# Chunk scores: levels computed on halves of TensorE's columns, both groups of heads in one step, scores kept head-innermost

## The chip, the core and the metric

One core of one Trainium2 chip runs the kernel. The metric is device time in microseconds, the median of several runs; one further execution was taken with the hardware profiler. Five engines work beside each other, each through its own queue in order: TensorE (PE, with its weight loads PEld), VectorE (DVE), ScalarE (ACT), GpSimd (POOL) and the queue engine SP. They wait for one another by semaphores.

## What is computed

One layer of a hybrid decoder: a gated linear recurrence (HGRN2) beside a gated short convolution, one output projection, then a gated MLP with a causal convolution. The change touches the recurrence's scores:

```python
def hgrn2_chunkwise(q, k, v, log_f):
    def step(state, inp):
        qc, kc, vc, gc = inp
        b = jnp.cumsum(gc, axis=-2)
        diff = b[..., :, None, :] - b[..., None, :, :]
        decay = jnp.exp(jnp.where(causal[:, :, None], diff, -jnp.inf))
        scores = jnp.einsum('bhtk,bhsk,bhtsk->bhts', qc, kc, decay)
        o = (jnp.einsum('bhts,bhsv->bhtv', scores, vc)
             + jnp.einsum('bhtk,bhkv->bhtv', qc * jnp.exp(b), state))
        ...
```

There are 4 heads of 128 features, 1024 tokens and 1024 model columns; everything is fp32.

## The kernel before

The 1024 tokens go through in two halves `hf` of 512, each half in four chunks of C = 128 tokens. The big products are split in two parts of a number (`hi`, `lo`, float32r) and done as three matmuls of 128x512 each (`mm3_fm`, `mm3_tm`, lines 177 to 185). A product of `gemm_quad` or `gemm_tile` is a run of such matmuls, and every 24 of them (or 12, by the `rate` argument) the helper `tick` takes one step out of the deque `fill` and records it there. So the scores and the recurrence (`score_steps`, `chunk_steps`) are recorded in small steps between the big matmuls. A scheduling layer then orders each engine's instructions; the order below is the one that it made.

`UW` holds keys and queries of the four chunks as (chunk parity `x`, key or query `s`, two groups `g` of four heads, token), `F` the decays, `S` the scores. Group g of parity x is chunk 2g + x. The scores are built without logarithms: `diag` (line 348) fills the diagonal, and then seven levels with block sizes h = 1, 2, 4, ... 64 (`LEVELS`) fill the blocks of h left tokens by h right tokens. Before each level `prepare` (line 364) gathers on ACT, into a tile `lhs`, the left keys of the even chunk and the right queries of the odd chunk, so that one matmul per head (line 380) serves both parities; the odd chunk's scores come out transposed. Then, on DVE: line 382 and line 384 multiply the blocks of `UW` with decays for the next level, line 386 merges the decays in `F`, and line 387 copies, where the mask `m_lev` says so, the wanted scores from PSUM into `S`. The next level's `prepare` needs lines 382 and 384, and its matmuls need `prepare`'s copy.

A level is done per group g: two steps `level(li, 0)` and `level(li, 1)`, each with its own matmuls (4 heads, 128 left columns by 128 moving columns), its own copies, and an `lhs` of 128x512 that has two buffers. So while one group's chain runs on DVE and ACT, the other group's matmuls and 12 to 24 big matmuls stand between on PE. After the levels, `scores` (in `chunk_steps`) transposes the odd chunks' scores by TensorE, and `output` multiplies scores and state with values and queries. PSUM tiles for all this come from a ring of four banks (`aux`). The masks are loaded by two DMAs on SP's queue and converted on POOL.

Of the kernel before, what the change touches and what calls it, by code (L numbers as in the profile page):

```python
# [38 lines left out]
N_MASK = C + C * len(LEVELS)  # L39
# [3 lines left out]
def decoder_kernel(ctx: ExitStack, tc: tile.TileContext, x, xT, w_sq, w_cv, w_out, w_up, w_dn,  # L43
# [24 lines left out]
    m_lev = zp.tile([P, len(LEVELS), 2, H, 64], U8, name="m_lev")  # L68
# [38 lines left out]
    def aux(name, shape=(P, TH)):  # L107
        return ps_ax.tile(list(shape), F32, tag="ax", name=name)
# [127 lines left out]
    S = zt("S", (P, 2, 8, C))  # L236
# [99 lines left out]
    def score_steps(hf, F, UW):  # L336
        kq = {}

        def products(xi, g):
            gs = slice(g * H, (g + 1) * H)  # L340
            p = cv(f"kq{hf}_{xi}_{g}", shape=(P, H, C))
            nc.vector.tensor_tensor(p[:], UW[:, 2 * xi, gs, :], UW[:, 2 * xi + 1, gs, :], ALU.mult)
            hi = cv(f"kqh{hf}_{xi}_{g}", F32R, (P, H, C))
            lo = cv(f"kql{hf}_{xi}_{g}", F32R, (P, H, C))
            split(p[:], hi[:], lo[:])
            kq[xi, g] = hi, lo

# [16 lines left out]
        def prepare(li, g):  # L364
            h = LEVELS[li]
            lhs = zt("lhs", (P, H, C), bufs=2, name=f"lhs{hf}_{li}_{g}")
            nc.scalar.copy(lhs.rearrange("p i (b two h) -> p (i b) two h", two=2, h=h),  # L367
                           view(UW, 4 * X, g * H * C, (2 * h, H * C // (2 * h)), (3 * X + h, 2), (1, h)))
            lhss[li, g] = lhs

        def level(li, g):
            h = LEVELS[li]
            nb = C // (2 * h)
            ps = aux(f"sl{hf}_{li}_{g}")
            lhs = lhss.pop((li, g))
            pv = ps.rearrange("p (x g b h) -> p x g b h", x=2, g=H, h=h)
            o, n = g * H * C, H * nb
# [3 lines left out]
            u = view(UW, 4 * X, o, (3 * X + h, 2), (2 * h, n), (1, h))  # L381
            nc.vector.tensor_tensor(u, u, view(F, 2 * X, o + h, (X - h, 2), (2 * h, n), (0, h)), ALU.mult)
            w = view(UW, 4 * X, X + o + h, (X - h, 2), (2 * h, n), (1, h))
            nc.vector.tensor_tensor(w, w, view(F, 2 * X, o, (X + h, 2), (2 * h, n), (0, h)), ALU.mult)  # L384
            left = view(F, 2 * X, o, (X, 2), (2 * h, n))
            nc.vector.tensor_tensor(left, left, view(F, 2 * X, o + h, (X, 2), (2 * h, n)), ALU.mult)
            nc.vector.copy_predicated(
                view(S, 2 * X, o + h, (X - h, 2), (2 * h, n), (1, h)),
                m_lev[:, li].rearrange("p x g (b h) -> p x (g b) h", h=h),
                ps.rearrange("p (x n h) -> p x n h", x=2, h=h))  # L390
# [8 lines left out]
        lg = [(li, g) for li in range(len(LEVELS)) for g in range(2)]  # L399

        steps = [chain((products, *xg[0]))] + [chain()] * (2 * hf)
        for i in range(4):
            steps.append(chain((diag, *xg[i]), *([(products, *xg[i + 1])] if i < 3 else []),
                               *([(prepare, 0, i // 2)] if i % 2 else [])))
        for li, g in lg:
            steps.append(chain((level, li, g), *([(prepare, li + 1, g)] if li + 1 < len(LEVELS) else [])))
# [5 lines left out]
    def chunk_steps(hf, F, UW, v, gg, ma):  # L412
        ma_hi, ma_lo = ma

        def make(c):
# [8 lines left out]
            def scores():  # L424
                ps = aux(f"so{n}", (P, H, C))
                for j, ph, _ in hs:
                    nc.tensor.transpose(ps[:, j, :], S[:, 1, ph, :], ident[:])
                nc.scalar.copy(S[:, 1, g * H : (g + 1) * H, :], ps[:])

            def output():  # L430
# [8 lines left out]
                for _, ph, js in hs:  # L439
                    if not first:  # L440
                        nc.tensor.matmul(po[:, js], Q[:, ph, :], st[0][:, js], start=True, stop=False)
                    nc.tensor.matmul(po[:, js], S[:, xi, ph, :], v[c][:, js], start=first, stop=True)
# [87 lines left out]
    def out_proj(hf, mix, gain, hooks=None):  # L530
# [46 lines left out]
        for nh in range(2):  # L577
            if nh and hf:
                for c in range(NC_H):
# [3 lines left out]
                            hooks=hooks if nh == 0 else None, rate=1 + (hf == 0))  # L583
# [81 lines left out]
    for i in range(2):  # L665
        mf = xslot(f"mf{i}")
        nc.sync.dma_start(mf[:], masks_d[:, i * TH : (i + 1) * TH])
        mv = mf.rearrange("p (l x n) -> p l x n", x=2, n=64)
        if i == 0:
            nc.gpsimd.tensor_copy(m_diag[:], mf[:, 0:C])  # L670
        for l in range(1 - i, 4):
            nc.gpsimd.tensor_copy(m_lev[:, 4 * i + l - 1], mv[:, l].unsqueeze(2).to_broadcast([P, 2, H, 64]))
# [14 lines left out]
    mix_a = mixers(0, act_a, F0, UW0, rb0, rq0, r0, ma_tiles(0), ((1, 2, 1, 2), (1, 2, 1, 2)), (2, 1, 2, 1, 2, 1, 2, 1, 2, 1, 2, 1),  # L687
# [14 lines left out]
    mix_b = mixers(1, act_b, F1, UW1, rb1, rq1, r1, ma_tiles(1), (2, 2), (1, 1, 1, 1, 1, 1, 1, 1, 1, 1, 2, 2))  # L702
# [510 lines left out]
```

## Time and profile before

| | us |
|---|---|
| median of 3 runs (1108.78 to 1110.8) | 1109.32 |
| profiled execution | 1109.08 |
| its span in the trace | 1107.3 |
| PE busy | 1095.9 |
| DVE busy | 826.9 |
| ACT busy | 514.3 |
| POOL busy | 14.0 |

The span is the time that the trace covers; some 1.8 us of the execution lie around it. A matmul is pipelined: its record lasts until its last result is modelled to have landed, so the records overlap, and what a matmul really takes is the distance from its start to the next one's start. An fp32 matmul is two records (two weight loads and two matmuls), a float32r matmul or an fp32 transpose one. A row "x8" merges eight records, with the first one's start and the time from there to the last one's end.

### The profile page before, as it was taken

What the parts mean: (1) busy time and instruction counts of PE and PEld (TensorE: products, weight loads), DVE (VectorE), ACT (ScalarE), POOL (GpSimd) and SP (SyncE); (2) the same over time, 40 slices, a digit from 0 to 9 for tenths busy, and PEclk for the clock granted to TensorE, in tenths of its full rate; (3) what the DMA queues carried; (4) which work ended last, traced back from release to release, by engine and by line L of the source; (5) the groups of instructions that cost most, each with busy time, mean ns of one, the idle gap of its engine ahead of it and who ended that gap; (6) DMA issues with size and microseconds to landing.
All of it is one profiled execution on the core that took longest, in us unless ns stands there. A gap on an engine that the chain in (4) does not pass through costs nothing.

```text
span 1107.3 us, 13513 instructions
## 1 busy us (share of the span) xinstructions
PE 1095.9 (99%) x5088; PEld 911.5 (82%) x5088; DVE 826.9 (75%) x1196; ACT 514.3 (46%) x769; POOL 14.0 (1%) x25
## 2 busy tenths in 40 slices
PE   9999999999999999999999999999999999999996
PEld 7888888887888888888888888888888888888885
DVE  7576877658954666388698888889888767855776
ACT  5543355433433337277444554445454434544541
POOL 2000000000000001000000000000000000000000
PEclk9999999999999999999999999999999999999999
DMA  9522223322352348075333333443432479877632
GB/s 297 193 95 76 77 76 126 116 98 70 101 185 96 96 131 271 27 256 176 128 130 137 133 124 128 157 162 107 158 115 86 136 257 408 319 249 234 208 105 107
DMA packets 56161, 170.38 MB, mean 154 GB/s; under 512 B 5656, under 2 KB 6176, under 8 KB 53152
## 3 DMA queue, kind: packets, MB, share of 16 engines
q1 hardware_dynamic: 54880, 165.50, 42.8%
q0 software_dynamic: 912, 3.67, 1.0%
q8 instruction: 40, 0.66, 0.2%
q10 hardware_dynamic: 304, 0.35, 0.1%
q14 instruction: 25, 0.20, 0.1%
HBM read 134.11 MB, written 35.39 MB: 153 GB/s over the span
## 4 chain that ended last, share of the span: by engine, by line
PE 94%; DVE 3%; issue 1%; ACT 1%; DMA 0%; DVEq 0%; SPq 0%; ACTq 0%
PE pG L178 7%; PE pG L180 7%; PE pG L179 7%; PE pV L178 4%; PE pV L180 4%; PE pV L179 4%; PE pX L183 3%; PE pX L185 3%; PE pX L184 3%; PE pY L183 3%; PE pY L184 3%; PE pY L185 3%; PE p_wo L183 2%; PE p_wo L184 2%; PE p_wo L185 2%; PE sl L380 2%
## 5 line engine op out<-in xcount | busy, mean ns | idle before, releaser
L117 DVE TENSOR_TENSOR ls<-s,hs 128x1024 fp32r<-128x1024 f32 (+1 forms) x40 | 45.1, 1129 | 46.1 <-ACT hs L116 46.1
L116 ACT CAST hs<-s 128x1024 fp32r<-128x1024 f32 (+1 forms) x40 | 39.1, 977 | 78.6 <-PE pY L184 28.8
L776 DVE TENSOR_TENSOR l_t<-t,h_t 128x1536 fp32r<-128x1536 f32 x22 | 38.6, 1754 | 32.3 <-ACT h_t L775 32.3
L775 ACT CAST h_t<-t 128x1536 fp32r<-128x1536 f32 x22 | 32.6, 1483 | 55.3 <-PE pG L179 55.3
L875 ACT ACTIVATE g<-g 128x1024 f32<-128x1024 f32 x22 | 23.4, 1062 | 64.8 <-DVE g L863 64.8
L185 PE MATMUL pY<-hw,ls 128*128 128x512 f32 x132 | 51.4, 389 | 0.0
L184 PE MATMUL pY<-lw,hs 128*128 128x512 f32 x132 | 51.3, 389 | 0.0
L183 PE MATMUL pY<-hw,hs 128*128 128x512 f32 x132 | 51.2, 389 | 0.0
L184 PE MATMUL pX<-lw,hs 128*128 128x512 f32 x116 | 45.1, 389 | 0.0
L183 PE MATMUL pX<-hw,hs 128*128 128x512 f32 x116 | 45.1, 389 | 0.0
L185 PE MATMUL pX<-hw,ls 128*128 128x512 f32 x116 | 45.1, 389 | 0.0
L367 ACT COPY lhs<-UW 128x512 f32<-128x512 f32 x28 | 18.6, 666 | 44.5 <-DVE UW L384 37.9
L861 ACT ACTIVATE g<-pG,vec 128x1024 f32<-128x1024 f32 x22 | 24.5, 1114 | 29.0 <-PE pG L180 29.0
L180 PE MATMUL pG<-uhi,l_x 128*128 128x512 f32 x96 | 37.4, 389 | 0.0
L178 PE MATMUL pG<-uhi,h_x 128*128 128x512 f32 x96 | 37.3, 389 | 0.0
L179 PE MATMUL pG<-ulo,h_x 128*128 128x512 f32 x96 | 37.3, 389 | 0.0
L862 DVE SCALAR_TENSOR_TENSOR g<-pG,vec,g 128x1023 f32<-128x1023 f32 x22 | 28.1, 1279 | 8.8 <-ACT g L861 8.8
L178 PE MATMUL pG<-c4h,h_b 128*128 128x512 f32 x88 | 34.3, 390 | 0.0
L179 PE MATMUL pG<-c4l,h_b 128*128 128x512 f32 x88 | 34.3, 390 | 0.0
L179 PE MATMUL pV<-c1l,h_t 128*128 128x512 f32 x88 | 34.3, 389 | 0.0
L178 PE MATMUL pV<-c1h,h_t 128*128 128x512 f32 x88 | 34.2, 389 | 0.0
L179 PE MATMUL pG<-c2l,h_t 128*128 128x512 f32 x88 | 34.2, 389 | 0.0
(361 smaller groups left out, 3410.1 us busy)
## 6 DMA issues: line engine op xcount, KB each, us to landing
w<-w_up SPq DMA_DIRECT2D x21, 1024.0 KB, 4.8
b<-w_dn SPq DMA_DIRECT2D x35, 512.0 KB, 7.1
s<-s_d SPq DMA_DIRECT2D x33, 512.0 KB, 6.2
s_d<-g SPq DMA_DIRECT2D x22, 512.0 KB, 2.7
s_d<-S SPq DMA_DIRECT2D x11, 768.0 KB, 3.4
r_wo<-w_out SPq DMA_DIRECT2D x16, 512.0 KB, 3.5
ah_w<-w_up SPq DMA_DIRECT2D x10, 512.0 KB, 4.9
f_d<-ah_f SPq DMA_DIRECT2D x9, 512.0 KB, 2.9
```

The lines of the kernel that those rows point to most:

```text
L116: nc.scalar.copy(hi, src)
L117: nc.vector.tensor_tensor(lo, src, hi.bitcast(F32), ALU.subtract)
L178: nc.tensor.matmul(ps, whi, ahi, start=first, stop=False, skip_group_check=more)
L179: nc.tensor.matmul(ps, whi, alo, start=False, stop=False, skip_group_check=more)
L180: return nc.tensor.matmul(ps, wlo, ahi, start=False, stop=last, skip_group_check=more)
L183: nc.tensor.matmul(ps, ahi, whi, start=first, stop=False, skip_group_check=more)
L184: nc.tensor.matmul(ps, ahi, wlo, start=False, stop=False, skip_group_check=more)
L185: return nc.tensor.matmul(ps, alo, whi, start=False, stop=last, skip_group_check=more)
L775: m = nc.scalar.copy(hi[:], src)
L776: casts[name] = m.ins, nc.vector.tensor_tensor(lo[:], src, hi[:].bitcast(F32), ALU.subtract).ins
L861: nc.scalar.mul(a[:], c, wc[2])
L862: nc.vector.scalar_tensor_tensor(a[:, 1:], c[:, : T - 1], wc[1], a[:, 1:], ALU.mult, ALU.add)
```

## The change

A level handles all 8 heads in one step. Its matmuls are cut in two: left columns 0 to 63 against the 64 moving columns that belong to them, and left columns 64 to 127 against theirs, each placed on its own half of the array's columns (`tile_position=(0, 0)` and `(0, 64)`), in alternation. So a level has 16 matmuls of 64 by 64 where two steps had 8 of 128 by 128. Their results land in PSUM with the head innermost, one column every 8 elements. `S` is (token, head) too, the masks are cut to half a row, and line 387's copy becomes two, one on each half of the partitions. For h = 64 the copy is two plain ones on ACT. `lhs` is one buffer of 128x1024. Before the odd chunks' transposes, three ACT copies per half put the scores back in head order (`even`, `odd`). The rates at which steps are taken are set anew: 12 score steps per half instead of 19 (without the empty ones).

```diff
-    m_lev = zp.tile([P, len(LEVELS), 2, H, 64], U8, name="m_lev")
+    m_lev = zp.tile([P, len(LEVELS) - 1, 2, W // 2, GH], U8, name="m_lev")
...
-    S = zt("S", (P, 2, 8, C))
+    S = zt("S", (P, 2, C, GH))
...
-            p = cv(f"kq{hf}_{xi}_{g}", shape=(P, H, C))
-            nc.vector.tensor_tensor(p[:], UW[:, 2 * xi, gs, :], UW[:, 2 * xi + 1, gs, :], ALU.mult)
+            p = cv(f"kq{hf}_{xi}_{g}", shape=(P, C, H))
+            nc.vector.tensor_tensor(
+                p.rearrange("p t i -> p i t"), UW[:, 2 * xi, gs, :], UW[:, 2 * xi + 1, gs, :], ALU.mult)
...
-        def prepare(li, g):
+        def prepare(li):
             h = LEVELS[li]
-            lhs = zt("lhs", (P, H, C), bufs=2, name=f"lhs{hf}_{li}_{g}")
...
+            lhss[li] = zt("lhs", (P, GH, C), name=f"lhs{hf}_{li}")
...
-            for i in range(H):
-                rhs = view(UW, 4 * X, X + o + i * C + h, (X - h, 2), (2 * h, nb), (1, h))
-                nc.tensor.matmul(pv[:, :, i], lhs[:, i, :], rhs, start=True, stop=True)
...
+            halves = [slice(w * W, (w + 1) * W) for w in range(2)]
+            for i in range(GH):
+                for w, ws in enumerate(halves):
+                    if h < W:
+                        rhs = view(UW, 4 * X, X + i * C + w * W + h, (X - h, 2), (2 * h, W // (2 * h)), (1, h))
+                    else:
+                        rhs = view(UW, 4 * X, X + i * C + (h, X)[w], (1, h))
+                    nc.tensor.matmul(ps[ws, ..., i], lhs[:, i, ws], rhs, start=True, stop=True, tile_position=(0, w * W))
...
+                    nc.vector.copy_predicated(
+                        to, m_lev[ws, li].rearrange("p x (b h) i -> p x b (h i)", h=h),
+                        ps[ws].rearrange("p x (b h) i -> p x b (h i)", h=h))
+                else:
+                    nc.scalar.copy(S[ws, w, (1 - w) * W : (2 - w) * W], ps[ws])
...
-        for li, g in lg:
-            steps.append(chain((level, li, g), *([(prepare, li + 1, g)] if li + 1 < len(LEVELS) else [])))
+        for li in range(len(LEVELS)):
+            steps.append(chain((level, li), *([(prepare, li + 1)] if li + 1 < len(LEVELS) else [])))
...
+                if c == 1:
+                    shared["even"] = zt("lhs", (P, GH, C), name=f"even{hf}")
+                    for gi in range(G):
+                        shared[gi] = cv(f"odd{hf}_{gi}", shape=(P, H, C))
+                        nc.scalar.copy(shared[gi].rearrange("p i t -> p t i"), S[:, 1, :, gi * H : (gi + 1) * H])
+                    nc.scalar.copy(shared["even"].rearrange("p i t -> p t i"), S[:, 0])
...
-        gg = evac_g(hf, gemm_quad(w_sq[3], act, f"g{hf}", True, PAIRS, rate=(2, 1, 2, 1)), r)
+        gg = evac_g(hf, gemm_quad(w_sq[3], act, f"g{hf}", True, PAIRS, rate=rates[1]), r)
...
-    mix_a = mixers(0, act_a, F0, UW0, rb0, rq0, r0, ma_tiles(0), ((1, 2, 1, 2), (1, 2, 1, 2)), (2, 1, 2, 1, 2, 1, 2, 1, 2, 1, 2, 1),
+    mix_a = mixers(0, act_a, F0, UW0, rb0, rq0, r0, ma_tiles(0), (1, (1, 1, 1, 2)), (1, 1, 1, 2, 1, 2, 1, 2, 1, 2, 2, 2),
...
-    mix_b = mixers(1, act_b, F1, UW1, rb1, rq1, r1, ma_tiles(1), (2, 2), (1, 1, 1, 1, 1, 1, 1, 1, 1, 1, 2, 2))
+    mix_b = mixers(1, act_b, F1, UW1, rb1, rq1, r1, ma_tiles(1), (1, 2), (1, 2, 1, 1, 2, 1, 1, 2, 1, 1, 2, 1))
```

How this moves instructions is shown at one place on three engines, the convolution stage of the first half. PE first (`sl` is the scores' PSUM tile, `p_ch` and `p_gb` are results of the convolution's products); before:

```order
L180 MATMUL p_ch_0_985<-hi_7_308,l_ch_0_981 128x512
L380 MATMUL sl_4_1_1010<-UW_392,lhs_4_1_963 128x2x64 x4
L178 MATMUL p_gb_0_1036<-hi_0_135,h_gb_0_1031 128x512
L179 MATMUL p_gb_0_1036<-lo_0_136,h_gb_0_1031 128x512
L180 MATMUL p_gb_0_1036<-hi_0_135,l_gb_0_1032 128x512
```

and now, where the sixth level comes in the same product:

```order
L182 MATMUL p_gb_0_1065<-lo_2_186,h_gb_0_1060 128x512
L183 MATMUL p_gb_0_1065<-hi_2_185,l_gb_0_1061 128x512
L387 MATMUL sl_5_1026<-UW_392,lhs_5_990 64x64 x16
L181 MATMUL p_gb_0_1065<-hi_3_206,h_gb_0_1060 128x512
L182 MATMUL p_gb_0_1065<-lo_3_207,h_gb_0_1060 128x512
```

A group of 4 has become one of 16, and the group stands inside a product instead of at its end. Between the levels of the first half stand 24, 26, 19, 19, 17 and 15 big matmuls now, in the second half 24, 24, 22, 22, 22 and 24 (and 6 more inside the level h = 8, after its ninth matmul). Before, from a group's level to its next, there were 24 to 48 and the other group's matmuls.

DVE at the levels h = 8 and 16 of the first half (`l_gc` is the low part of a weight, `gc` the convolution's gate); before:

```order
L492 TENSOR_TENSOR gc_0_976<-gc_0_976,rb_368 128x512
L382 TENSOR_TENSOR UW_392<-UW_392,F_115 128x2x32x8
L387 COPY_PREDICATED S<-m_lev,sl_3_1_954 128x2x32x8
L384 TENSOR_TENSOR UW_392<-UW_392,F_115 128x2x32x8
L117 TENSOR_TENSOR l_gc_1_1090<-r_gc_1_1088,h_gc_1_1089 128x1024
L386 TENSOR_TENSOR F_115<-F_115 128x2x32
L387 COPY_PREDICATED S<-m_lev,sl_4_0_965 128x2x16x16
```

and now:

```order
L389 TENSOR_TENSOR UW_392<-UW_392,F_115 128x2x64x8
L399 COPY_PREDICATED S<-m_lev,sl_3_905 64x2x4x64
L391 TENSOR_TENSOR UW_392<-UW_392,F_115 128x2x64x8
L399 COPY_PREDICATED S<-m_lev,sl_3_905 64x2x4x64
L393 TENSOR_TENSOR F_115<-F_115 128x128
L513 TENSOR_TENSOR gc_0_992<-p_gc_0_943,rb_368 128x512
L389 TENSOR_TENSOR UW_392<-UW_392,F_115 128x2x32x16
```

The multiplications are twice as long and a score copy stands between the two that the next `prepare` needs; there is no second group's work between the levels. ACT at the same place, before:

```order
L116 CAST h_gb_0_1031<-r_gb_0_1030 128x1024
L367 COPY lhs_4_0_913<-UW_392 128x512
L116 CAST h_gc_1_1089<-r_gc_1_1088 128x1024
L367 COPY lhs_4_1_963<-UW_392 128x512
L367 COPY lhs_5_0_974<-UW_392 128x512
L116 CAST h_ch_1_1132<-r_ch_1_1131 128x1024
```

and now:

```order
L119 CAST h_gb_0_1060<-r_gb_0_1059 128x1024
L371 COPY lhs_3_891<-UW_392 128x1024
L119 CAST h_gc_1_1118<-r_gc_1_1117 128x1024
L371 COPY lhs_4_927<-UW_392 128x1024
L119 CAST h_ch_1_1170<-r_ch_1_1169 128x1024
L371 COPY lhs_5_990<-UW_392 128x1024
```

Each level has one `prepare` of double width, with a weight's cast between two of them.

## Rows read from the trace of the kernel before

**Rows 1.** The page: span, busy time of each engine with its share of the span, the granted clock of TensorE in 40 slices (9 is full), and the shares of the chain that ended last.

```profile
span 1107.3 us, 13513 instructions
PE 1095.9 (99%) x5088; PEld 911.5 (82%) x5088; DVE 826.9 (75%) x1196; ACT 514.3 (46%) x769; POOL 14.0 (1%) x25
...
PEclk9999999999999999999999999999999999999999
...
PE 94%; DVE 3%; issue 1%; ACT 1%; DMA 0%; DVEq 0%; SPq 0%; ACTq 0%
```

**Rows 2.** The view of waits, for PE: who waited for whom, us in total, times, the longest.

```profile
PE sl L380 <- DVE UW L384: 1.4, 4, 0.4
PE pw L80 <- DVE pr L497: 1.0, 1, 1.0
PE pZ L184 <- DVE lw L117: 0.5, 1, 0.5
```

**Rows 3.** PE's timeline around the first level group of the first half: start, time to the end of the last record, line, output<-inputs, weights' rows*columns, shape.

```profile
74.28 0.39 PE L184 MATMUL p_i<-l_i,hi 128*128 128x512 f32 x1
74.51 0.39 PE L185 MATMUL p_i<-h_i,lo 128*128 128x512 f32 x1
74.73 1.07 PE L380 MATMUL sl<-UW,lhs 128*128 128x128 f32 x8
75.56 0.48 PE L183 MATMUL p_g<-h_g,hi 128*128 128x512 f32 x1
75.87 0.40 PE L184 MATMUL p_g<-l_g,hi 128*128 128x512 f32 x1
76.11 0.40 PE L185 MATMUL p_g<-h_g,lo 128*128 128x512 f32 x1
...
296.07 1.05 PE L380 MATMUL sl<-UW,lhs 128*128 128x128 f32 x8
```

**Rows 4.** The tile `sl`: all its weight loads and matmuls, with duration ns min/median/max.

```profile
L380 PEld LDWEIGHTS sl<-UW,lhs x224: 186/191/192, 74.5 to 307.6; 128*128 128x128 f32 x112
L380 PE MATMUL sl<-UW,lhs x224: 270/275/353, 74.7 to 307.7; 128*128 128x128 f32 x112
```

**Rows 5.** PE's timeline at the statistics of the first half: eight records with 128 weight columns and one moving column (`pc<-ones,acc`), and a transpose whose weights are 4 columns (`pc<-ident,rs_x`), which the program places on a strip of 32 columns of the array. Then the line of that transpose, with its weight load.

```profile
29.26 0.39 PE L180 MATMUL p_q<-hi,l_q 128*128 128x512 f32 x1
29.49 0.95 PE L649 MATMUL pc<-ones,acc 128*128 128x1 f32 x8
30.30 0.49 PE L178 MATMUL p_q<-hi,h_q 128*128 128x512 f32 x1
30.62 0.40 PE L179 MATMUL p_q<-lo,h_q 128*128 128x512 f32 x1
...
32.48 0.40 PE L178 MATMUL p_q<-hi,h_q 128*128 128x512 f32 x1
32.71 0.27 PE L279 MATMUL pc<-ident,rs_x 128*4 128x128 f32 x1
32.74 0.47 PE L179 MATMUL p_q<-lo,h_q 128*128 128x512 f32 x1
33.05 0.39 PE L180 MATMUL p_q<-hi,l_q 128*128 128x512 f32 x1
...
L279 PEld LDWEIGHTS pc<-ident,rs_x x1: 83/83/83, 32.5 to 32.5; 128*4 128x4 f32 x1
```

**Rows 6.** The timeline of all engines from one level group (h = 8, group 0 of the first half) to the next `prepare`; in brackets the idle time before, and who ended it.

```profile
102.92 1.05 PE L380 MATMUL sl<-UW,lhs 128*128 128x128 f32 x8
103.73 0.48 PE L178 MATMUL p_gc<-hi,h_gc 128*128 128x512 f32 x1
...
104.01 0.69 DVE L382 TENSOR_TENSOR UW<-UW,F 128x512 f32<-128x512 f32 x1 [2.94 <-PE sl L380]
104.62 0.70 DVE L387 COPY_PREDICATED S<-m_lev,sl 128x512 f32<-128x512 uint8 x1
105.22 0.68 DVE L384 TENSOR_TENSOR UW<-UW,F 128x512 f32<-128x512 f32 x1
105.82 1.22 DVE L117 TENSOR_TENSOR l_gb<-r_gb,h_gb 128x1024 fp32r<-128x1024 f32 x1
105.99 0.62 ACT L367 COPY lhs<-UW 128x512 f32<-128x512 f32 x1 [1.24 <-DVE UW L384]
106.95 0.26 DVE L386 TENSOR_TENSOR F<-F 128x64 f32<-128x64 f32 x1
```

**Rows 7.** The timeline where PE waited for a level's operands.

```profile
81.66 0.39 PE L184 MATMUL p_g<-l_g,hi 128*128 128x512 f32 x1
81.79 0.69 DVE L384 TENSOR_TENSOR UW<-UW,F 128x512 f32<-128x512 f32 x1
81.89 0.39 PE L185 MATMUL p_g<-h_g,lo 128*128 128x512 f32 x1
82.63 1.15 PE L380 MATMUL sl<-UW,lhs 128*128 128x128 f32 x8 [0.36 <-DVE UW L384]
```

**Rows 8.** Single lines: duration ns min/median/max of DVE's multiplications and score copies (the longest of line 387 are those of h = 1 and 2), and of ACT's copies and casts.

```profile
L357 DVE TENSOR_TENSOR UW<-UW,F x4: 1218/1224/1226, 57.8 to 250.0; 128x1024 f32<-128x1024 f32 x4
L387 DVE COPY_PREDICATED S<-m_lev,sl x28: 699/732/1309, 76.5 to 309.3; 128x512 f32<-128x512 uint8 x28
L367 ACT COPY lhs<-UW x28: 612/621/872, 59.3 to 301.9; 128x512 f32<-128x512 f32 x28
L428 ACT COPY S<-so x4: 570/581/585, 138.1 to 355.5; 128x512 f32<-128x512 f32 x4
L116 ACT CAST h_gc<-r_gc x8: 1045/1045/1055, 89.3 to 380.5; 128x1024 fp32r<-128x1024 f32 x8
```

**Rows 9.** Stretches of time: busy us of PE, PEld, DVE, ACT and POOL (instructions), granted clock, DMA share, GB/s. The two stretches hold the levels of the first and of the second half.

```profile
74.00:137.00 63.00, 62.64 (x329) 52.99 (x329) 48.35 (x75) 21.99 (x30) 0.00 (x0) 1.00 0.23 76
257.00:308.00 51.00, 49.97 (x273) 42.27 (x272) 46.88 (x83) 21.15 (x41) 0.00 (x0) 1.00 0.30 98
```

More of the change, by code (lines that the diff above doesn't have):

```diff
@@ L38 @@
 V_N = V_FCONV + 3 * 2 * NF
-N_MASK = C + C * len(LEVELS)
+G = 2
+GH = G * H
+W = C // 2
+N_MASK = C + W * (len(LEVELS) - 1)
 @with_exitstack
@@ new lines, in prepare, with level @@
+            lhss[li] = zt("lhs", (P, GH, C), name=f"lhs{hf}_{li}")
+            nc.scalar.copy(lhss[li].rearrange("p i (b two h) -> p (i b) two h", two=2, h=h),
+                           view(UW, 4 * X, 0, (2 * h, X // (2 * h)), (3 * X + h, 2), (1, h)))
+        def level(li):
+            h = LEVELS[li]
+            n = X // (2 * h)
+            ps = aux(f"sl{hf}_{li}", (P, 2, W // 2, GH) if h < W else (P, W, GH))
+            lhs = lhss.pop(li)
+            halves = [slice(w * W, (w + 1) * W) for w in range(2)]
[6 more added lines that the diff above has]
+                    nc.tensor.matmul(ps[ws, ..., i], lhs[:, i, ws], rhs, start=True, stop=True, tile_position=(0, w * W))
+            u = view(UW, 4 * X, 0, (3 * X + h, 2), (2 * h, n), (1, h))
+            nc.vector.tensor_tensor(u, u, view(F, 2 * X, h, (X - h, 2), (2 * h, n), (0, h)), ALU.mult)
+            w = view(UW, 4 * X, X + h, (X - h, 2), (2 * h, n), (1, h))
+            nc.vector.tensor_tensor(w, w, view(F, 2 * X, 0, (X + h, 2), (2 * h, n), (0, h)), ALU.mult)
+            left = view(F, 2 * X, 0, (X, 2), (2 * h, n))
+            nc.vector.tensor_tensor(left, left, view(F, 2 * X, h, (X, 2), (2 * h, n)), ALU.mult)
+            for w, ws in enumerate(halves):
+                if h < W:
+                    sv = S[ws]
+                    to = bass.AP(tensor=sv.tensor, offset=sv.offset + (w * W + h) * GH,
+                                 ap=[list(sv.ap[0]), [X - h * GH, 2], [2 * h * GH, W // (2 * h)], [1, h * GH]])
+                    nc.vector.copy_predicated(
[3 more added lines that the diff above has]
+                    nc.scalar.copy(S[ws, w, (1 - w) * W : (2 - w) * W], ps[ws])
@@ L403, in score_steps @@
             steps.append(chain((diag, *xg[i]), *([(products, *xg[i + 1])] if i < 3 else []),
[L404 to L406 removed]
+                               *([(prepare, 0)] if i == 3 else [])))
+        for li in range(len(LEVELS)):
+            steps.append(chain((level, li), *([(prepare, li + 1)] if li + 1 < len(LEVELS) else [])))
         return steps
@@ L441, in output @@
                         nc.tensor.matmul(po[:, js], Q[:, ph, :], st[0][:, js], start=True, stop=False)
-                    nc.tensor.matmul(po[:, js], S[:, xi, ph, :], v[c][:, js], start=first, stop=True)
+                    nc.tensor.matmul(po[:, js], shared[("even", "odd")[xi]][:, ph, :], v[c][:, js], start=first, stop=True)
                 ssq = small(f"sso{n}")
```

68 lines of the change are left out of this document (23 added, 45 removed).

## The prediction

> **What bounds the kernel now.** I read the page first: PE is busy for 1095.9 of 1107.3 us at the full clock, and the chain that ended last is 94% PE [rows 1]. Then the waits of PE, longest first: the top of the list is 1.4 us, and it is the levels' matmuls that waited for DVE's second multiplication; the next are 1.0 and 0.5 [rows 2]. So PE hardly ever stands still, and every microsecond of TensorE work that goes or comes is a microsecond of the kernel, unless a new wait takes its place. Third, PE's timeline around one level group: what it costs, from start to start. Fourth, the score stages' stretches, to see how much room DVE has: 48.35 busy of 63 us in the first half and 46.88 of 51 in the second [rows 9], 77% and 92%. ACT has 21.99 and 21.15, so it is not short of room. The profiled execution is 1109.08 us against the median of 1109.32, so I work out a difference and take it from 1109.3.
>
> **Level matmuls, removed.** A group of eight records starts at 74.73 and the next matmul at 75.56: 0.83 us. That next one takes 0.31 to its successor (75.56 to 75.87) where the ordinary step is 0.23 (74.51 less 74.28): 0.08 more [rows 3]. 28 groups x 0.91 = 25.5 us, all on PE and so all on the path.
>
> **Level matmuls, added.** 14 levels of 16 matmuls, 32 records each. What does a record of 64 columns by 64 take? Within a group the starts of the seven steps lie (1.07 - 0.275) / 7 = 0.114 us apart [rows 3, 4]. Eight records with a single moving column stand equally close, 0.81 us in all against 0.83 [rows 5], so it is the load of 128 weight columns that sets this pace, at least as much as the stream of 128 moving ones. A load of 4 columns lasts 83 ns, one of 128 lasts 191 [rows 4, 5]: 0.87 ns a column, so 64 columns fewer save 0.056 us and a record stands alone at about 0.058 us. The moving columns are halved too.
>
> The open question is whether the two halves of the array work side by side. The trace has no two matmuls on different columns, so I bound it by the rows above. Fully side by side, two records pass in 0.058: 31 x 0.029 + 0.03 (the step to the next matmul, 0.83 - 7 x 0.114) + 0.08 = 1.01 us a level, 14.1 us in all, **a gain of 11.4**. In turns: 31 x 0.058 + 0.11 = 1.91 a level, 26.7 us, a loss of 1.2. I take side by side: the change alternates the halves record pair by record pair, left and right have their own weights, moving columns and PSUM partitions, and already now loads and matmuls overlap freely (a load of 191 ns every 114).
>
> Two things could add to a record. The first is changing between the whole array and halves, 28 times. The 4-column transpose stands on a strip of 32 columns between whole-array matmuls: from the matmul before it to the second behind it are 0.57 us (32.48 to 33.05), of which two ordinary steps are 0.45; the 0.12 left is what a load-paced record of 0.114 costs [rows 5]. So no price of changing is seen, and the sum has none. The Trainium skill, TensorEngine Tiling (Array Packing), section Tiling Modes, says the contrary: a change of the tiling mode drains the engine. By it the gain would shrink to 6.9; that is rival A.
>
> The second is the write to PSUM, one column every 8 elements. No matmul here writes at a step. The nearest rows: reading the moving columns in steps of 2 (h = 1) costs nothing, 1.07 against 1.05 us for a group [rows 3]; but DVE's predicated copy into `S` in runs of 1 or 2 elements takes 1309 ns where longer runs take 699 [rows 8], a factor of 1.87. So the factor lies between 1 and 1.87, and I take 1, since the rows on PE itself are the nearer ones. The Trainium skill, PSUM — Partial Sum Buffer, section Specifications (TRN2), speaks against it: PSUM has lines of 8 bytes and a pattern that is not contiguous slows matmuls significantly, without a figure. No run here shows it; it is part of rival C.
>
> **The chain between levels.** With one `lhs` buffer and no second group, a level's matmuls must wait for: first multiplication, a score copy, second multiplication, `prepare`. From the start of the big matmul behind a level (103.73): 0.28 to DVE's start (104.01) [rows 6]; a multiplication of 1024 wide 1.22 alone [rows 8], 1.13 when the next follows (105.82 to 106.95), a copy 0.60 (104.62 to 105.22), 0.09 from DVE's end to ACT (105.90 to 105.99) [rows 6], a copy of 1024 on ACT 1.04 as the cast of that width [rows 8], and 0.15 from the last operand to the matmul (82.48 to 82.63) [rows 7]. 0.28 + 1.13 + 0.60 + 1.22 + 0.09 + 1.04 + 0.15 = 4.5 us. PE has N big matmuls in the meantime, N x 0.227 (two ordinary steps are 74.28 to 74.73 [rows 3], 0.45) + 0.09: 5.5 us at 24, 4.4 at 19, 3.9 at 17, 3.5 at 15 (there the order has no copy between, so 3.9 are needed). In the first half that leaves waits of about 0.1, 0.1, 0.6 and 0.4. At two places, one in each half, ACT does an evacuation that waits for the last quarter of a product ahead of the `prepare`, some 0.2 and 0.6; at the second half's first level DVE has a weight's low part ahead, 0.3, and at its last a residual's step and a low part between the multiplications, 0.2. Together 2.5 us against 1.4 now: **a loss of about 1.1**. Behind the waiting matmul the whole of PE's queue waits, so all of it counts. The upper end: if each of the 12 passages finds DVE or ACT in one more 1.22 us instruction, it is 14.6 more. The lower end is none at all, a gain of 1.4.
>
> **What I cost at nothing.** DVE's work shrinks: 28 score copies of 0.89 become 24 of about 0.73, 56 multiplications of 0.69 become 28 of 1.22; it eases the 92% and shows only in the waits above. The copies `even` and `odd` lie between the last level and the transposes: 0.28 + 2 x 0.58 + 1.04 + 0.62 + 0.15 = 3.3 us [rows 8] beside 24 big matmuls of 5.5; without that cover it would be 3.3 a half. `products` writing in steps and the diagonal's copy in runs of 4 are on DVE ahead of matmuls that now come 24 apart instead of 12. The masks are one transfer fewer on SP's queue, and POOL is busy for 14.0 us in all [rows 1]. Transposes, big matmuls and `output` are as many as before.
>
> **Sum:** 1109.3 - 11.4 + 1.1 = 1099.0.
>
> **Rivals.** *A, every change of the array's division empties the pipeline.* A record lasts 0.39 where the step is 0.23, so emptying costs 0.16 [rows 3]; 28 x 0.16 = 4.5, which gives 1103.5. Against it speaks the 4-column transpose [rows 5]. For it speaks the rule of the Trainium skill named above. *B, the halves take turns* (one path for the weights, which the load-paced records make possible): +1.2 + 1.1 gives 1111.6, just at the edge of what can be told from no change. *C, the stepped write costs 1.87.* A record is then 0.108; side by side 31 x 0.054 + 0.11 = 1.78 a level, 25.0 us, and the time 1109.9, no change; in turns 3.46 a level, 48.4 us, and 1133.3, slower. The factor turns the sign in turns at once, side by side only at about 1.8. *D, the chain becomes the bound and it ends slower*: the 12 passages each 1.22 us late, 1099.0 + 14.6 = 1113.6. It decides from 0.9 us per passage on. Against it speaks that ACT is half idle and DVE gets easier; for it, that in the second half DVE is 92% busy and both queues are strictly in order.
>
> **How the numbers follow.** The measurement can tell some 0.2%, 2.2 us, from no change. Forecast (1096 to 1102) 0.52; A 0.10, faster as well; B 0.16, half of it within 2.2 us and half slower; C side by side 0.07, same; C in turns 0.07, slower; D 0.08, slower. So faster 0.62, same 0.15, slower 0.23. The range reaches from 1096, full overlap with no waits left (1109.3 - 11.4 - 1.4 = 1096.5), to 1112, which takes in A, B and C side by side, and leaves out C in turns, most of D and some rest, under 0.2.
>
> **What the profile after would show.** Right: the level's records in 448 pieces, a level's first start to the next big matmul 0.9 us, PE's waits for `sl` 2 to 3 us, span near 1097. Rival A: the first record of a level or the first big matmul behind it 0.16 later. B: 1.8 us a level, starts 0.058 apart. C: starts wider than 0.058 at h < 64 and h = 64 alike, and 1.7 or 3.4 a level. D: level time as forecast, but waits of `sl` above 10 us in the view of waits. I am wrong altogether if the big matmuls' step of 0.227 changes or if new idle time stands at `so` or `sd`.

## The result, and the profile after

The changed kernel takes 1100.27 us, median of 6 runs (1099.83 to 1102.43), against 1109.32 (1108.59 to 1110.86, 6 runs). The ratio is 0.9918 with a 95% interval of 0.9905 to 0.9931: faster by 0.8%, 9.05 us. The forecast was 1099.0. The profiled execution has a span of 1098.0 us against 1107.3 [rows 1]. On the page, PE again fills its span and the clock is full in all slices:

```profile
span 1098.0 us, 13874 instructions
PE 1087.5 (99%) x5312; PEld 900.7 (82%) x5312; DVE 821.5 (75%) x1150; ACT 521.3 (47%) x765; POOL 13.5 (1%) x24
...
PE 96%; DVE 3%; issue 0%; ACT 0%; DMA 0%; DVEq 0%; SPq 0%; ACTq 0%
```

PE's 1095.9 became 1087.5: the gain is TensorE time, as forecast. How a level looks now, in PE's timeline at h = 8 of the first half (start, time to the end of the last record, line, output<-inputs, weights' rows*columns, shape):

```profile
104.44 0.39 PE L182 MATMUL p_gc<-lo,h_gc 128*128 128x512 f32 x1
104.67 0.39 PE L183 MATMUL p_gc<-hi,l_gc 128*128 128x512 f32 x1
104.98 1.15 PE L387 MATMUL sl<-UW,lhs 128*64 128x64 f32 x32
106.06 0.50 PE L181 MATMUL p_gc<-hi,h_gc 128*128 128x512 f32 x1
106.40 0.39 PE L182 MATMUL p_gc<-lo,h_gc 128*128 128x512 f32 x1
```

Read the starts. 32 records of 64 columns take 1.08 us (104.98 to 106.06), where eight of 128 took 0.83 [rows 3]: 1.08 / 16 = 0.068 for two of half the width, where one whole one took 0.114. Whether that is two halves side by side or just shorter records, e1 tests. Inside the level the trace has the second record of a pair 0.007 behind the first, and a pair every 0.058 us, which is the pace that the forecast took. But the step from the last large matmul into the level is 0.31 (104.67 to 104.98) where an ordinary one is 0.23 and where the first record of a group used to follow at 0.22 [rows 3]; and the large matmul behind takes 0.34 to its successor, where it took 0.31. By the starts a level costs 0.09 + 1.08 + 0.11 = 1.28 us, not the 1.01 of the forecast.

The waits of PE in the score stages, in the same columns as [rows 2]:

```profile
PE p_i L186 <- DVE m_o L550: 0.4, 1, 0.4
PE sl L387 <- ACT lhs L371: 0.4, 1, 0.4
```

The four waits of `sl` for the second multiplication, 1.4 us in all, became one of 0.4 for `lhs`; new is one of `p_i` for a PSUM bank that DVE had not emptied. The trace's starts, summed over the levels' stretches (what lies between a large matmul and the second one behind the level, less its ordinary steps), give 27.9 us before and 19.5 after: 8.4 of the 9.2 by which the spans of the two profiled executions differ. Of the rest, 0.3 stand at the start of the program (its first product is that much earlier) and 0.5 elsewhere.

Most kernels here have single executions that are some 2 us longer than their others (before 1110.8, after 1102.4; the last section shows what two of them are), so a median of few runs can move by a microsecond, and I read the traces' starts beside it.

### The profile page after: what moved, and what is told of

It is laid out like the page before. It is cut to its first block, busy times and chain, and to the rows that moved or that the text cites. A ratio compares the mean times of both kernels' runs of the same rounds, so it can differ in the third digit from the quotient of the medians.

```text
span 1098.0 us, 13874 instructions
## 1 busy us (share of the span) xinstructions
PE 1087.5 (99%) x5312; PEld 900.7 (82%) x5312; DVE 821.5 (75%) x1150; ACT 521.3 (47%) x765; POOL 13.5 (1%) x24
## 4 chain that ended last, share of the span: by engine, by line
PE 96%; DVE 3%; issue 0%; ACT 0%; DMA 0%; DVEq 0%; SPq 0%; ACTq 0%
PE pG L181 7%; PE pG L183 7%; PE pG L182 7%; PE pV L181 4%; PE pV L183 4%; PE pV L182 4%; PE pX L188 3%; PE pX L186 3%; PE pX L187 3%; PE pY L186 3%; PE pY L187 3%; PE pY L188 3%; PE p_wo L186 3%; PE p_wo L188 2%; PE p_wo L187 2%; PE pA L183 2%
## 5 line engine op out<-in xcount | busy, mean ns | idle before, releaser
L183 PE MATMUL pG<-c4h,l_b 128*128 128x512 f32 x88 | 34.3, 390 | 0.0
L181 PE MATMUL pV<-c3h,h_b 128*128 128x512 f32 x88 | 34.3, 390 | 0.0
L183 PE MATMUL pV<-c1h,l_t 128*128 128x512 f32 x88 | 34.3, 390 | 0.0
L181 PE MATMUL pG<-c2h,h_t 128*128 128x512 f32 x88 | 34.3, 390 | 0.0
```

Source lines behind the costliest of these rows:

```text
L181: nc.tensor.matmul(ps, whi, ahi, start=first, stop=False, skip_group_check=more)
L183: return nc.tensor.matmul(ps, wlo, ahi, start=False, stop=last, skip_group_check=more)
```

## The experiments

Theory at the outset: halves side by side, and each entry into halves with its return costs a fixed 0.25 to 0.35 us. Rivals: such a price doesn't exist, and the long steps are data that arrive just in time; the gain comes from having half as many passages; the stepped write costs something.

**e1, in turns.** The same matmuls, in another order:

```diff
-            for i in range(GH):
-                for w, ws in enumerate(halves):
+            for w, ws in enumerate(halves):
+                for i in range(GH):
```

Expected: 

> The kernel after, but a level's sixteen matmuls go in another order: first the eight heads on the left half of the array, then the eight on the right half. My theory is that neighbours on different halves run side by side (a pair of records passes every 0.059 us in the trace after) and that two records on the same half cannot. Then the 32 records of a level are about 0.058 apart, a level takes some 2.0 to 2.2 us instead of 1.28, and the kernel 10 to 13 us more than after: 1110 to 1113. The rival is that the load of 64 weight columns sets the pace of each record by itself and the halves have no part in it: then nothing changes, 1100.3, starts 0.029 apart on average.

Measured: 1110.08, ratio to before 1.0009 [1.0000, 1.0018]. In its timeline, the same level:

```profile
109.18 0.39 PE L183 MATMUL p_gc<-hi,l_gc 128*128 128x512 f32 x1
109.50 1.90 PE L387 MATMUL sl<-UW,lhs 128*64 128x64 f32 x32
111.33 0.50 PE L181 MATMUL p_gc<-hi,h_gc 128*128 128x512 f32 x1
111.67 0.39 PE L182 MATMUL p_gc<-lo,h_gc 128*128 128x512 f32 x1
```

1.83 us in place of 1.08: 0.057 a record, where in alternation a pair takes 0.058. Neighbours on different halves pass side by side, neighbours on the same half one after the other. Without this order of the two loops nothing of the gain is left. The steps in and out of the level (0.32, 0.34) are what they were.

**e2, halves alone; e3, both groups in one step alone.** Two parts of the change, each on the kernel before. e2, for the 24 groups below h = 64 (the score copies follow in two or four pieces):

```diff
-                nc.tensor.matmul(pv[:, :, i], lhs[:, i, :], rhs, start=True, stop=True)
...
+                for w in range(2):
+                    ws, bs = slice(w * 64, w * 64 + 64), slice(w * nb // 2, (w + 1) * nb // 2)
+                    rhs = view(UW, 4 * X, X + o + i * C + w * 64 + h, (X - h, 2), (2 * h, nb // 2), (1, h))
+                    nc.tensor.matmul(pv[ws, :, i, bs], lhs[:, i, ws], rhs, start=True, stop=True, tile_position=(0, w * 64))
...
```

e3, with the numbers of steps that the change gives to each product:

```diff
-        for li, g in lg:
-            steps.append(chain((level, li, g), *([(prepare, li + 1, g)] if li + 1 < len(LEVELS) else [])))
+        for li in range(len(LEVELS)):
+            more = li + 1 < len(LEVELS)
+            steps.append(chain(*[f for g in range(2) for f in [(level, li, g)] + [(prepare, li + 1, g)] * more]))
...
```

Expected of e2: 

> The kernel before, and of the change only the halves: the levels h = 1 to 32 of each group of heads on halves of the array's columns, group by group as before (24 of the 28 groups, 16 records each), scores in the layout of before, copied in two or four pieces on 64 partitions. My theory is that each entry into halves and each return costs, together 0.25 to 0.34 us, whatever number of matmuls lies between. A group then takes 0.09 + 0.47 + 0.15 + 0.11 = 0.82 us against 0.92: 24 x 0.10 = 2.3 us gained, about 1107. The rival, the forecast's own sum without such a price: 15 x 0.029 + 0.11 = 0.55 a group, 24 x 0.37 = 8.9 gained, about 1100.4. DVE has more copies (four of 128 columns in place of one of 512), which can bring waits of up to 2 us.

Expected of e3: 

> The kernel before, and of the change only the step: both groups of heads in one step, in the places that the change gives its steps, matmuls on the whole array, scores in the layout of before. My theory is that this gains hardly anything on TensorE: sixteen records of 0.112 in a row and one return, 1.82 us, against two groups of 0.92: 14 x 0.02 = 0.3 us, and the waits for the multiplications change by 1 or 2 us either way: 1107 to 1111. The rival is that the gain of the whole change came from having half as many passages between levels: then it is near 1100.

Measured: e2 1105.77, ratio 0.9969 [0.9957, 0.9981]; e3 1111.27, ratio 1.0021 [1.0012, 1.0031]. A group of e2 in PE's timeline:

```profile
101.70 0.39 PE L185 MATMUL p_g<-h_g,lo 128*128 128x512 f32 x1
102.02 0.69 PE L386 MATMUL sl<-UW,lhs 128*64 128x64 f32 x16
102.63 0.50 PE L178 MATMUL p_gc<-hi,h_gc 128*128 128x512 f32 x1
102.97 0.39 PE L179 MATMUL p_gc<-lo,h_gc 128*128 128x512 f32 x1
```

and one of the five levels of e3 that run in one piece:

```profile
126.66 0.39 PE L180 MATMUL p_gb<-hi,l_gb 128*128 128x512 f32 x1
126.89 1.95 PE L380 MATMUL sl<-UW,lhs 128*128 128x128 f32 x16
128.59 0.48 PE L178 MATMUL p_gc<-hi,h_gc 128*128 128x512 f32 x1
128.91 0.40 PE L179 MATMUL p_gc<-lo,h_gc 128*128 128x512 f32 x1
```

e2's group costs 0.09 + 0.61 + 0.11 = 0.81 against 0.91: 0.61 where the matmuls took 0.83, but the entry and the return eat half of that gain. Its 24 x 0.10 = 2.4 us are near the 3.1 measured and far from the 8.9 of a sum without the price.

e3 did less than its edit asks for: in nine of the 14 levels the scheduling layer left 3 to 10 large matmuls between the two groups (at h = 4 of the first half they start at 101.61 and 103.58, with four between). A level in one piece costs 1.70 + 0.09 = 1.79, which is two groups of 0.90, and gains nothing. By the starts the levels' stretches hold 30.2 us against 27.9, and the difference is waits. So the step alone is tested at five levels, and there it is worth nothing.

The two parts give -3.1 and +2.4, and the whole change -9. What they do together shows between e2 and the kernel after, whose levels' stretches hold 24.6 and 19.5 us: in the levels below h = 64 twelve entries are paid in place of 24, and each saves 2 x 0.81 - 1.28 = 0.35, 4.2 in all; h = 64, which e2 leaves whole, brings 4 x 0.90 - 2 x 1.28 = 1.0. The waits of e3 don't come in the kernel after; why was not tested.

**e4, the write to PSUM without a step.**

```diff
-                    nc.tensor.matmul(ps[ws, ..., i], lhs[:, i, ws], rhs, start=True, stop=True, tile_position=(0, w * W))
+                    to = ps[ws].rearrange("p x c i -> p (x c i)" if h < W else "p c i -> p (c i)")[:, i * W : (i + 1) * W]
+                    nc.tensor.matmul(to, lhs[:, i, ws], rhs, start=True, stop=True, tile_position=(0, w * W))
```

Expected: 

> The kernel after, but each level matmul writes its 64 columns to PSUM side by side instead of one every 8 elements. The copies are left as they are, so they put scores into other places of S than the reference has them. The forecast took a price of 1 for the step (rival C: up to 1.87). If the step is free, as the pace of 0.059 a pair says (64 columns are the same at h = 1 and at h = 64, all at a step of 8), the time stays at 1100.3 and a pair at 0.059. If the step costs even 20% of a pair, 16 x 14 x 0.010 = 2.2 us come off and the time is 1098.

Measured: 1101.53 (1099.99 to 1102.19), ratio 0.9924 [0.9908, 0.9941]. Its scores land in other places than the layer needs, so only its time is of use. The same level:

```profile
106.96 0.39 PE L183 MATMUL p_gc<-hi,l_gc 128*128 128x512 f32 x1
107.28 1.15 PE L388 MATMUL sl<-UW,lhs 128*64 128x64 f32 x32
108.36 0.50 PE L181 MATMUL p_gc<-hi,h_gc 128*128 128x512 f32 x1
```

1.08 us from the first record to the next large matmul, as in the kernel after. A write of one column every 8 elements costs TensorE nothing here; rival C is out.

**e5 and e6, the price by itself.** One whole-array matmul of 512 columns more in each level, in its middle (e5) or behind it (e6, with `GH - 1` for `H - 1`):

```diff
+                if i == H - 1:
+                    extra = aux(f"ex{hf}_{li}", (P, 4, P))
+                    nc.tensor.matmul(extra[:], ones_r[:], ones_r[:].unsqueeze(1).to_broadcast([P, 4, P]), start=True, stop=True)
```

Expected of e5: 

> The kernel after, with one additional matmul of 512 columns on the whole array (ones by ones, its result is not read) in the middle of each of the 14 levels, between the eighth and the ninth of the sixteen matmuls. My theory is that each entry into halves and each return costs, together 0.3 us: the additional matmul costs its own 0.227 and one more entry and return, 14 x (0.227 + 0.3) = 7.4 us, about 1107.7, and 4.2 us more than the same matmul at the end of the level. The rival is that there is no such price and the long steps ahead of a level and behind it are data that arrive just in time: then it costs 14 x 0.227 = 3.2, about 1103.5, like the next kernel.

Expected of e6: 

> The control of the run before: the kernel after with the same additional matmul behind the sixteenth matmul of each level, where the whole-array matmuls go on anyway. Both theories: 14 x 0.227 = 3.2 us, about 1103.5, less up to 0.5 where a wait becomes shorter since the passage to the next level is longer.

Measured: e5 1107.62, e6 1103.41, ratios 0.9983 [0.9974, 0.9992] and 0.9951 [0.9937, 0.9966]. PE's timeline of e5:

```profile
105.70 0.39 PE L183 MATMUL p_gc<-hi,l_gc 128*128 128x512 f32 x1
106.02 0.69 PE L387 MATMUL sl<-UW,lhs 128*64 128x64 f32 x16
106.64 0.50 PE L390 MATMUL ex<-ones_r 128*128 128x512 f32 x1
107.07 0.69 PE L387 MATMUL sl<-UW,lhs 128*64 128x64 f32 x16
107.68 0.50 PE L181 MATMUL p_gc<-hi,h_gc 128*128 128x512 f32 x1
108.02 0.39 PE L182 MATMUL p_gc<-lo,h_gc 128*128 128x512 f32 x1
108.25 0.40 PE L183 MATMUL p_gc<-hi,l_gc 128*128 128x512 f32 x1
```

and of e6:

```profile
104.71 0.39 PE L182 MATMUL p_gc<-lo,h_gc 128*128 128x512 f32 x1
105.03 1.15 PE L387 MATMUL sl<-UW,lhs 128*64 128x64 f32 x32
106.11 0.50 PE L390 MATMUL ex<-ones_r 128*128 128x512 f32 x1
106.45 0.39 PE L183 MATMUL p_gc<-hi,l_gc 128*128 128x512 f32 x1
106.68 0.40 PE L181 MATMUL p_gc<-hi,h_gc 128*128 128x512 f32 x1
106.91 0.40 PE L182 MATMUL p_gc<-lo,h_gc 128*128 128x512 f32 x1
```

Both stretches hold the same records and four large steps: 105.70 to 108.25 is 2.55 us, 104.71 to 106.91 is 2.20. The same matmul in the middle costs 0.35 us more. Nothing had to be waited for there (`lhs` is the same one, `ones_r` is constant): this is the price of leaving the halves and coming back. In e6 one level came in two pieces (22 and 10 records, with a wait between), so e5 has 13 entries more: 13 x 0.35 = 4.5. Less some 0.8 of waits at that level of e6, and 0.3 by which e6's first product runs later, 3.4 are left; the profiled executions lie 3.2 apart (1106.48 and 1103.33), the medians 4.2.

**e8, the evacuation that came too late.** The four m_o evacuations of the first output projection's second block get a higher priority (`tc.high_priority()` around the line).

Expected: 

> The kernel after, with the four last evacuations m_o of the first output projection put ahead in DVE's queue. In the trace after the fourth of them stands behind the multiplications of a level, and the matmuls of p_i wait for its PSUM bank: 0.16 and 0.58 us, with a level broken in two by it, which costs one more entry and return, 0.3. If this is right, about 1.0 us goes; but the second multiplication of the level h = 2 comes up to 1.2 us later, and the wait of the level h = 4 for its lhs, 0.42 now, may grow by as much. So 1099.3 to 1100.5, and in the trace no wait of p_i for m_o, and fourteen levels in one piece each.

Measured: 1099.76 (1099.04 to 1100.89), ratio 0.9916 [0.9901, 0.9930]; not to be told from the kernel after. In the trace it did what was said: all levels in one piece, no wait of `p_i`, two waits of `sl` (0.5 in all), 18.6 us by the starts in the levels' stretches where the kernel after has 19.5. What it gained is within the spread.

**e7, e9, e11: quarters.** If side by side pays, four strips of 32 columns should pay more, for the levels whose blocks fit (h up to 16):

```diff
-            ps = aux(f"sl{hf}_{li}", (P, 2, W // 2, GH) if h < W else (P, W, GH))
+            W = C // (4 if h < 32 else 2)
+            ps = aux(f"sl{hf}_{li}", (P, 2, W // 2, GH) if h < 64 else (P, W, GH))
...
-            halves = [slice(w * W, (w + 1) * W) for w in range(2)]
+            halves = [slice(w * W, (w + 1) * W) for w in range(C // W)]
...
-                        to, m_lev[ws, li].rearrange("p x (b h) i -> p x b (h i)", h=h),
+                        to, m_lev[ws, li, :, (w * W % 64) // 2 : (w * W % 64 + W) // 2].rearrange("p x (b h) i -> p x b (h i)", h=h),
```

Expected: 

> The kernel after with the levels h = 1 to 16 on quarters of the array: per head four matmuls of 32 weight columns by 32 moving columns, four strips side by side, four score copies of 32 partitions by 256 in place of two of 64 by 512; h = 32 and 64 stay on halves. If four records on four strips pass in the time that the stream of 32 columns takes, half of the 0.052 us of 64 columns and three short steps of 0.007, a quad needs 0.045 at most and a level 16 x 0.047 + 0.34 = 1.09 in place of 1.28: ten levels, 1.9 us less, 1098.4; at best 16 x 0.03: 4.6 less. The rival: a matmul takes a fixed time of some 0.029 to be started, whatever its size; then 64 records need 1.9 us and the ten levels cost 9 us more, 1109. DVE has 0.3 to 0.5 us more of copies a level, which may add waits of 1 us in the second half.

Measured: 1105.59 (1102.56 to 1105.73), ratio 0.9961 [0.9947, 0.9975]: slower than the kernel after, though PE's timeline shows the level cheaper:

```profile
97.27 0.39 PE L187 MATMUL p_g<-l_g,hi 128*128 128x512 f32 x1
97.58 0.76 PE L388 MATMUL sl<-UW,lhs 128*32 128x32 f32 x64
98.28 0.50 PE L188 MATMUL p_g<-h_g,lo 128*128 128x512 f32 x1
98.61 0.39 PE L186 MATMUL p_g<-h_g,hi 128*128 128x512 f32 x1
```

64 records in 0.70 us, against 32 in 1.08: 0.011 a record, so the rival's fixed 0.029 is out. With the steps in and out a level costs 0.31 - 0.23 + 0.70 + 0.10 = 0.88, where 1.09 was expected and 0.82 at best. The gain, 0.39 a level by the trace, went into waits of PE and, behind the longest of them, into 1.6 us at the lower clock (last section):

```profile
PE sl L388 <- ACT lhs L371: 4.2, 5, 1.9
...
PE p_i L187 <- DVE l_i L120: 1.2, 1, 1.2
PE p_i L186 <- DVE m_o L551: 0.8, 1, 0.8
```

e9 puts the copies behind the second multiplication in DVE's queue and m_o early; e10 does the same to the kernel after:

```diff
-            nc.vector.tensor_tensor(w, w, view(F, 2 * X, 0, (X + h, 2), (2 * h, n), (0, h)), ALU.mult)
+            last = nc.vector.tensor_tensor(w, w, view(F, 2 * X, 0, (X + h, 2), (2 * h, n), (0, h)), ALU.mult)
...
+                    with tc.issue_after(last.ins):
```

Expected of e9: 

> The quarters again, with two edits for the waits that they brought: the score copies of a level stand behind the second multiplication in DVE's queue, so that a copy of 0.44 us no longer lies in the chain to the next level, and the last evacuations m_o of the first output projection stand early as in e8. In the trace of the quarters a level took 0.39 us less on TensorE than on halves, 10 x 0.39 = 3.9, and new waits of some 7 us took it back. If these waits came from the length of the chain on DVE, 1.6 to 2 us are left of them here: 1096.5 to 1099. If DVE is the bound in these stretches by its sum of work (four copies of 0.44 in place of two of 0.73), the waits stay: 1102 and more.

Expected of e10: 

> The same two edits on the kernel after, with halves at all levels. The trace after has only 1.2 us of waits in the score stages, e8 had 0.8, so at most 1 us can go: 1099.3 to 1100.3.

Measured: e9 1099.20, ratio 0.9914 [0.9900, 0.9927]; e10 1101.36 (1099.72 to 1102.09), ratio 0.9925 [0.9913, 0.9938], no difference to the kernel after that could be told. Part of the waits went; 3.5 us of waits for `lhs` are left in e9, all in passages of 16 to 19 large matmuls. e11 gives all six passages of the first half 24 (the products of `g` issue one step a block, the convolution's take over the others), with the copies behind as in e9 and m_o where it was; e12 does it with halves, copies behind and m_o early.

```diff
-    mix_a = mixers(0, act_a, F0, UW0, rb0, rq0, r0, ma_tiles(0), (1, (1, 1, 1, 2)), (1, 1, 1, 2, 1, 2, 1, 2, 1, 2, 2, 2),
+    mix_a = mixers(0, act_a, F0, UW0, rb0, rq0, r0, ma_tiles(0), (1, (1, 1, 1, 1)), (1, 1, 1, 1, 2, 2, 1, 2, 2, 2, 2, 2),
```

Expected of e11: 

> The quarters with the score copies behind the second multiplication, and the steps of the first half spread so that all six passages between its levels hold 24 matmuls of 512 (e9: 24, 21, 17, 19, 16, 23); the second half's hold 22 to 26; m_o stands as in the kernel after. In e9 all waits for lhs, 4.3 us by the starts, stood in passages of 16 to 19 matmuls, 3.7 to 4.4 us, none in those of 20 and more. If the chain of two multiplications, a low part or copy, and prepare needs 4.5 to 5.1 us, 24 matmuls (5.5 us) cover it, nearly all of it goes, and the time is 1099.2 - 3.5 = 1095.5 to 1096.5. If DVE's sum of work is the bound, the waits come back at other places, 1099.

Expected of e12: 

> The same spread of the steps with halves at all levels, with the copies behind and m_o early as in e10: the control of e11. The waits of e10 are 1.1 us by the starts; at most 1 us goes: 1099 to 1100. The difference to e11 is then what the quarters bring by themselves, 10 x 0.39 = 3.9 us.

Measured: e11 1096.77 (1096.57 to 1098.29), ratio to before 0.9891 [0.9873, 0.9908]; e12 1099.25 (1098.77 to 1101.03), ratio 0.9912 [0.9897, 0.9928]. In e11's view of waits, none of `sl` is left; the m_o that stayed where it was costs 1.0:

```profile
PE p_i L186 <- DVE m_o L552: 1.0, 2, 0.8
```

By the starts its levels' stretches hold 15.0 us against e12's 18.6: 3.6 of the 3.9 that ten levels should give. The medians differ by 2.5; in the traces e11's first product is 0.6 later, and its transposes wait 0.3 for the copies `odd`. e11 is the fastest version here, 12.2 us below the kernel before; over the kernel after it leads by 3.5 in the medians, in different sets of runs, and the interval of each ratio is 1.4 to 2 us to either side.

## Why the prediction held, point by point

- **Bound, sign and mechanism: right.** PE is the bound before and after, the levels' matmuls are where the time went, and the halves run side by side (e1). Rival B would have been the time of e1. Rival D's sign, waits of `sl` above 10 us, isn't there: 0.4.
- **Level matmuls, removed: right.** 25.5 forecast; by the starts a group that waits for nothing costs 0.90 to 0.91.
- **Level matmuls, added: the term that was mis-sized.** 1.01 us a level forecast, 1.28 measured. The step that failed is "no price of changing is seen, and the sum has none". It was read from one 4-column transpose [rows 5] and carried over to matmuls on halves; e5 and e6 show 0.35 us for one return and entry, 0.27 more than the 0.08 that the forecast allows. The pace of the records was right, 0.058 a pair, so the price is the whole miss: 14 x 0.27 = 3.8 us of the forecast gain of 11.4 were never there. The prediction had named the sign: 0.9 from a level's first start to the next large matmul if it was right, 0.16 more under rival A. The 1.08 is rival A's sign, and its 2 x 0.16 a level is near the measured price. The Trainium skill, TensorEngine Tiling (Array Packing), section Tiling Modes, says that a change of the mode drains TensorE. With rival A's 0.16 a change, an estimate from [rows 3], the added term would have been 14 x 1.33 = 18.6; measured are 14 x 1.28 = 17.9. That the price is a draining is not shown: by the records, whose ends are modelled, a level's first record starts at 104.98 while the last large one runs to 105.06 (104.67 + 0.39). Why the transpose of [rows 5] paid nothing stays open. The Trainium skill, TensorEngine Tiling (Array Packing), Restrictions under Tile-to-Partition Mapping, says that column tiling disables the transpose mode for FP32. By that the transpose may not have run as an instruction on a strip, and was then no witness; no run here shows it.
- **Stepped write, factor 1: right** (e4). The Trainium skill, PSUM — Partial Sum Buffer, section Specifications (TRN2), expects a slow-down of matmuls by a pattern that isn't contiguous. The measurement differs and decides: the level took 1.08 us with and without the step.
- **The chain between levels: 4.5 us right in length, its waits too high.** At h = 8 the next large matmul starts at 106.06 and the next level at 110.60: 4.54 us with 19 matmuls between, no wait where 0.1 was forecast. The price itself lies in the passage: its steps in and out (0.09 + 0.11) lengthen PE's work by 0.2 while the chain runs. And at h = 16 and 32 the 0.28 to DVE's start doesn't exist. In the timeline of the level h = 16:

```profile
110.60 1.15 PE L387 MATMUL sl<-UW,lhs 128*64 128x64 f32 x32
111.68 0.50 PE L182 MATMUL p_ch<-lo,h_ch 128*128 128x512 f32 x1
...
111.18 1.22 DVE L389 TENSOR_TENSOR UW<-UW,F 128x1024 f32<-128x1024 f32 x1
```

  the first multiplication starts 0.50 before the next large matmul; it writes only what `prepare` had read. The forecast waits of the first half, 0.1 + 0.1 + 0.6 + 0.4, all came out as nought. In the second half 0.4 at `lhs` was forecast as 0.6; the multiplication of a residual and low parts cost nothing, but the fourth evacuation m_o, behind a level's chain in DVE's queue, held `p_i` back and broke a level in two, which the forecast had not seen:

```profile
284.13 0.80 PE L387 MATMUL sl<-UW,lhs 128*64 128x64 f32 x18
285.34 0.50 PE L186 MATMUL p_i<-h_i,hi 128*128 128x512 f32 x1 [0.42 <-DVE m_o L550]
...
286.92 0.68 PE L387 MATMUL sl<-UW,lhs 128*64 128x64 f32 x14
```

  By the starts the waits at the levels went from about 2.4 us to 1.2 (the views, which leave out short ones, count 1.4 and 0.8), so the term was -1.2 in place of +1.1.
- **What was cost at nothing: right only because it was covered.** `even` and `odd` write at a step, and ACT's copies took 2.08 and 1.18 us, where 1.04 and 0.58 had been read from plain copies: 4.4 us a half in place of 2.2, and ACT's busy time rose from 514.3 to 521.3. That the step is the reason was not tested. The 24 large matmuls in front of the transposes hid it here; in e11 0.3 of it shows.
- **The sum.** -11.4 + 1.1 was forecast. Measured: the matmuls 17.9 - 25.5 = -7.6, a fifteenth entry by the broken level +0.35, waits -1.2, the start and elsewhere -0.8: about -9.3, against -9.2 in the profiles and -9.05 in the medians. Two errors of 3.8 and 2.3 stood against each other; that the time came out 1.3 us from the forecast is in part luck.

## What to carry to other kernels

Small matmuls that fill half or a quarter of the array's columns pay if neighbours in the queue sit on different strips, and if enough of them stand together: on Trainium2 an entry and return cost 0.35 us in these runs, so gather them before dividing. When TensorE's work shrinks, the chain of the other engines behind it is next; count the matmuls that cover each passage, and spread the steps until the shortest passage is longer than the chain. A price read from one unusual instruction is no price for another kind: bound it from both sides and put the nearer rival into the sum.

## What the runs showed of the hardware

Each halving of the columns brings records about twice as close: inside a level the starts lie 0.111 us apart for a whole record (e3), 0.058 for a pair on halves (after) and 0.034 for four on quarters (e7). The steps in and out don't shrink with them: 0.32 ahead and 0.33 to 0.34 behind in both.

A wait can cost twice. In e7 PE stood idle for most of 287.3 to 291.3 (busy 0.20 of 2.0 us and 0.76 of 2.0); right behind it the granted clock is 0.50, that is 1.2 GHz. Nine steps from 291.93 to 295.57 take 3.64 us, where nine of 0.227 are 2.04: 1.6 us more. Stretches with busy us and instructions of PE, PEld, DVE, ACT and POOL, granted clock, DMA share, GB/s:

```profile
287.30:289.30 2.00, 0.20 (x1) 0.00 (x0) 1.91 (x4) 2.00 (x2) 0.00 (x0) 1.00 0.00 0
289.30:291.30 2.00, 0.76 (x64) 0.65 (x64) 1.96 (x4) 0.05 (x1) 0.00 (x0) 1.00 0.00 0
292.20:295.00 2.80, 2.80 (x8) 2.15 (x7) 2.67 (x6) 0.88 (x1) 0.00 (x0) 0.50 0.60 187
```

TensorE's clock rises at different times at the start of the program, and that is worth up to 2 us. e4's profiled execution took 1102.19 us, though its levels cost what the kernel after's cost; PE's timeline at the start of its first product:

```profile
6.27 0.79 PE L181 MATMUL p_f<-hi,h_f 128*128 128x512 f32 x1 [1.02 <-DVE l_f L143]
...
8.07 0.63 PE L181 MATMUL p_f<-hi,h_f 128*128 128x512 f32 x1
8.50 0.63 PE L182 MATMUL p_f<-lo,h_f 128*128 128x512 f32 x1
...
10.35 0.40 PE L181 MATMUL p_f<-hi,h_f 128*128 128x512 f32 x1
10.59 0.40 PE L182 MATMUL p_f<-lo,h_f 128*128 128x512 f32 x1
```

Steps of 0.43 in place of 0.23, as in e7 at a granted clock of 0.50, and they end where the trace's first clock record begins: at 10.0 us in e4, and in the same way at 10.4 in e1, whose profiled execution is the longest of its ten. In the kernel after that record begins at 6.2, in e11 at 4.3. (The views show 1.00 also for the time ahead of it, where the trace has no record.) So TensorE stood at its lower level, 1.2 GHz, for some 4 us longer in e4 than in the kernel after. The 21st matmul of the first product starts at 12.88 in e4 and at 10.59 in the kernel after, 2.3 us apart, which is nearly all of the 2.4 between the two executions. What lets the clock rise late is not shown: e2's first product starts as late as e1's (5.77 and 5.75), and its record begins at 5.1. For executions without a trace none of this is shown.
